# A hybrid attention layer on one core: the order of the two gated branches and the spread of the quarter sums

## The chip, the cores and the metric

The kernel runs on one core of a Trainium2 chip. The metric is the device time of one execution in microseconds, the median of the runs.

## The reference, cut to what matters

One layer of a streaming encoder for two request groups, 1024 prompt tokens and 32 sample tokens, all in fp32, with D = 1024:

```python
h = rms_norm(x, g_pre_mix)
qa, ka, va, ra, alr, qb, kb, vb, ga, gb = split_cols(h @ w_in)
oa, s_gla = gla_branch(qa, ka, va, ra, alr, ...)      # 4 heads, gated recurrence, width 1024
ob, k_rows, v_rows = attn_fn(qb, kb, vb, rel_bias)    # 8 heads, banded softmax, width 512
mix = (sigmoid(ga) * (oa @ w_br_a) + sigmoid(gb) * (ob @ w_br_b)) @ w_out
x = x + rms_norm(mix, g_post_mix)
f, conv_new = conv_ffn(rms_norm(x, g_pre_ffn), ...)
x = x + rms_norm(f, g_post_ffn)
gate = sigmoid(rms_norm(x, g_pre_ple) @ w_ple_gate)
x = x + rms_norm(gate * (pe @ w_ple), g_post_ple)
```

The change concerns the `mix` line, and a preparation for the products `h @ w_in` of the merge gates ga and gb.

## The kernel before, in words

**Products.** Everything is held with the features on the partitions, and the T = 1056 tokens along the free axis in three chunks of 352. An fp32 product is made of three TensorE passes on rounded halves: each operand is split into a high part (a copy to fp32r on ScalarE) and a low part (the difference, on VectorE or GpSimd), and `product` (L230 to L236) issues high x high (L234), low x high (L235) and high x low (L236). `split_hi_lo` (L238 to L240) splits activations: L239 on ScalarE, L240 on VectorE. `weights` (from L200) loads one weight tile of 512 KB into `raw` (L204, two buffers, issued by SP) and splits it in two halves, L213 on ScalarE and L214 on GpSimd, into four buffers each of `whi` and `wlo`, so that two weight tiles are alive.

**Order of work.** The program is written in one order, and a scheduler with a time model of its own orders the instructions of each engine, within the limits of the buffers. `tc.keep_in_program_order` pins an instruction; `low(QLOW)` gives a piece of work a low priority, `hp_if` a high one. Each engine takes its instructions strictly in order, and so does SP, which issues nearly all loads and stores: a DMA whose buffer or data is not ready holds up all that SP has behind it.

**Head pairs.** The band attention goes over four pairs of heads (loop `for hp in range(4)`, L706 on). In each, TensorE alternates between projection matmuls and the steps of the attention: scores (`two`, L550, L551), bias and the row's extreme on VectorE (L557), exponentials on ScalarE (L559), transposes (`one`, L566), their split on ScalarE (L569) and VectorE (`pt`, L570), the product with the values (`one`, L608) and its evacuation (L575). `vs` (L506) are the value rows, and `qs` (L525, L526) the split queries, whose low half GpSimd makes.

**Quarter sums.** The merge gates are computed later by a Strassen-Winograd scheme of seven products in place of eight, which needs sums of quarters of h. `quarter_sums(k)` (L681 to L704) makes them for one k of four: for each of two halves ten VectorE instructions on 128 x 264 tiles and four stores (L691, L696, L700, L704) from `tt` tiles to the DRAM tensor `d_t`. `tt` has four buffers. The table QUARTERS says after which head pair which k is made: k = 0 and 1 in the third, 2 and 3 in the fourth. They have low priority and so fill VectorE beside the attention.

**Branch stage.** It follows the merge gates, whose last matmuls end at 876.7 us of the span. `bh`, `bl` are the split halves of ob; `oa0h`, `oa0l` to `oa7h`, `oa7l` are those of oa, the low tile being loaded with the raw oa from DRAM (`d_oa`) first. Only oa0h to oa2h have room ahead of time; oa3h to oa7h lie in a pool `op` that opens when `bh` and `bl` are released. `ev` is a pool of five buffers of 128 x 1056, on which everything that comes and goes draws.

- Branch B: eight tiles n, each three chunks of four inner steps, two tiles to one weight tile. The gate d_gb[n] is loaded into an ev buffer (L1221), multiplied in on VectorE out of PSUM (L1226) and the result stored to DRAM, `d_tb` (L1227). The loads of oa (L1229) stand behind these stores by the table OA_LOADS.
- The splits of oa, chunk by chunk (L239, L240 again).
- Branch A: eight tiles n, each three chunks of eight inner steps, one weight tile each. The gate d_ga[n] (L1257) and the B result d_tb[n] (L1258) are loaded into two ev buffers; VectorE multiplies by the gate (L1269) and adds B (L1270), and the sum is split into `mh` and `ml` (L239, L240), the operand of w_out. Tile 0 is done in two parts, three inner steps for all chunks first.
- After each A tile comes `presplit(n)` (L1242 to L1249): it loads a tile of w_ple_gate (L1245), splits it on ScalarE (L1246) and VectorE (L1247), and stores both halves to the DRAM tensor `d_g` (L1248, L1249) for the end of the kernel. It takes two ev buffers.

PSUM has four buffers (`mm`) for these products, so TensorE can run up to three chunks ahead of an evacuation that is late. Then comes the stage of w_out, chunk by chunk, with mh and ml as its operands, its inner step 7 needing tile 7.

Of the kernel before, what the change touches and what calls it, by code (L numbers as in the profile page):

```python
# [11 lines left out]
F32 = mybir.dt.float32  # L12
# [5 lines left out]
P = 128  # L18
# [31 lines left out]
MS = 1  # L50
EVB = 5
QN = 2
QUARTERS = ((), (), (0, 1), (2, 3))
QLOW = 300
SLOTS = 7
LOOK = 2
PLAIN_GATES = (2, 3, 4, 5, 6, 7)
FIRST_SUMS = (2, 2, 2, 2, 4, 4, 0)
XB = 8
# [56 lines left out]
def emit(tc, a):  # L116
# [12 lines left out]
    def tl(p, shape, dt=F32, tag=None, bufs=None):  # L129
        tag = tag or nm("t")  # L130
        kw = {} if bufs is None else {"bufs": bufs}
        return p.tile(list(shape), dt, name=nm(tag), tag=tag, **kw)
# [17 lines left out]
    def ps_mm():  # L150
        return tl(psum, [P, 512], tag="mm", bufs=banks[0])
# [12 lines left out]
    def evt():  # L164
        return tl(ev, [P, T], tag="ev", bufs=EVB)
# [34 lines left out]
    def weights(src, eng=po, parts=1):  # L200
        raw = raw_weight()
        n = KT // parts
        for i in range(0, KT, n):
            dma.dma_start(raw[:, i : i + n], src[:, i : i + n])  # L204
        n = min(n, KT // 2)
        hi, lo = [], []
        with tc.high_priority():
            for i in range(0, KT, n):
                if i % (KT // 2) == 0:
                    hi.append(tl(wp, [P, KT // 2, P], F32R, tag="whi", bufs=4))  # L210
                    lo.append(tl(wp, [P, KT // 2, P], F32R, tag="wlo", bufs=4))
                b, d = slice(i, i + n), slice(i % 4, i % 4 + n)
                ac.activation(hi[-1][:, d], raw[:, b], AF.Copy)  # L213
                eng.tensor_tensor(lo[-1][:, d], raw[:, b], hi[-1][:, d], op=ALU.subtract)  # L214
        return hi, lo
# [19 lines left out]
            pe.matmul(ps, h, xl(kt), start=False, stop=False)  # L235
            pe.matmul(ps, l, xh(kt), start=False, stop=(last and i == n - 1))  # L236

    def split_hi_lo(hi, lo, src):  # L238
        ac.activation(hi, src, AF.Copy)  # L239
        ve.tensor_tensor(lo, src, hi, op=ALU.subtract)  # L240

    def log_exp():
        tc.keep_in_program_order(ac.preload_act_table_set("natural_log_exp_and_others"))
# [437 lines left out]
    def quarter_sums(k):  # L681
        a1, a2, b1, b2 = [[t[:, r].bitcast(F32) for t in (xh, xl)] for r in (k, k + HK) for _ in range(2)]
        n = HT // QN
        for j in range(QN):
            p, q = slice(j * n, (j + 1) * n), slice(HT + j * n, HT + (j + 1) * n)
            A, S = ALU.add, ALU.subtract
            t = tl(bp, [P, n], tag="tt", bufs=4)
            tc.keep_in_program_order(ve.tensor_tensor(t, a2[0][:, q], a1[0][:, p], op=S))
            ve.tensor_tensor(t, t, a2[1][:, q], op=A)
            ve.tensor_tensor(t, t, a1[1][:, p], op=S)  # L690
            dma.dma_start(d_t[0, k][:, p], t)  # L691
            t = tl(bp, [P, n], tag="tt", bufs=4)
            ve.tensor_tensor(t, b2[0][:, q], a2[0][:, q], op=S)
            ve.tensor_tensor(t, t, b2[1][:, q], op=A)
            ve.tensor_tensor(t, t, a2[1][:, q], op=S)
            dma.dma_start(d_t[2, k][:, p], t)  # L696
            u = tl(bp, [P, n], tag="tt", bufs=4)
            ve.tensor_tensor(u, t, a1[0][:, p], op=A)
            ve.tensor_tensor(u, u, a1[1][:, p], op=A)
            dma.dma_start(d_t[1, k][:, p], u)  # L700
            t = tl(bp, [P, n], tag="tt", bufs=4)
            ve.tensor_tensor(t, b1[0][:, p], u, op=S)
            ve.tensor_tensor(t, t, b1[1][:, p], op=A)
            dma.dma_start(d_t[3, k][:, p], t)  # L704
# [505 lines left out]
    banks[:] = [MODE, 8 - MODE, 0]  # L1210
    ps_one()

    OA_LOADS = ((), (0,), (1,), (2,), (3, 4), (5,), (6, 7), ())
    d_tb = tl(dram, [8, P, T], tag="d_tb")
    for n2 in range(4):
        hi, lo = weights(a["w_br_b"][n2])
        gs = {}
        for i in range(2):
            n = 2 * n2 + i
            g = evt()  # L1220
            dma.dma_start(g, d_gb[n])  # L1221
            for c in range(NC):
                s = chunk(c)
                ps = ps_mm()[:, : s.stop - s.start]
                product(ps, hi, lo, [(4 * i + k, k) for k in range(4)], lambda k: bh[:, k, s], lambda k: bl[:, k, s])
                ve.tensor_tensor(g[:, s], ps, g[:, s], op=ALU.mult)  # L1226
            dma.dma_start(d_tb[n], g)  # L1227
            for kt in OA_LOADS[n]:
                tc.keep_in_program_order(dma.dma_start(oa[kt][1].bitcast(F32), d_oa[kt]))  # L1229
    bo.release()  # L1230

    op = pool("op", side="right")
    for kt in range(3, KT):
        oa[kt][0] = tl(op, [P, T], F32R, tag=f"oa{kt}h")
    for c in range(NC):
        for kt in range(KT):
            h, l = [t[:, chunk(c)] for t in oa[kt]]
            with hp_if(c == 0):
                split_hi_lo(h, l, l.bitcast(F32))
    d_g = tl(dram, [KT, 2, P, KT, P], tag="d_g")  # L1240

    def presplit(n):  # L1242
        raw, hi = evt(), tl(ev, [P, T], F32R, tag="ev", bufs=EVB)
        raw, hi = raw[:, : KT * P], hi[:, : KT * P]
        dma.dma_start(raw.rearrange("p (k c) -> p k c", c=P), a["w_ple_gate"][n])  # L1245
        ac.activation(hi, raw, AF.Copy)  # L1246
        ve.tensor_tensor(raw.bitcast(F32R), raw, hi, op=ALU.subtract)  # L1247
        dma.dma_start(d_g[n, 0].rearrange("p k c -> p (k c)"), hi.bitcast(F32))  # L1248
        dma.dma_start(d_g[n, 1].rearrange("p k c -> p (k c)"), raw)  # L1249

    mp = pool("mp")
    mh = tl(mp, [P, KT, T], F32R, tag="mh")
    ml = tl(mp, [P, KT, T], F32R, tag="ml")
    for n in range(KT):
        hi, lo = weights(a["w_br_a"][n])
        g, t = evt(), evt()
        dma.dma_start(g, d_ga[n])  # L1257
        dma.dma_start(t, d_tb[n])  # L1258
        parts = [range(KT)] if n else [range(3), range(3, KT)]
        mms = [ps_mm()[:, : width(c)] for c in range(NC)] if n == 0 else []  # L1260
        for ks in parts[:-1]:
            for c in range(NC):
                s = chunk(c)
                product(mms[c], hi, lo, [(k, k) for k in ks], lambda k: oa[k][0][:, s], lambda k: oa[k][1][:, s], last=False)
        for c in range(NC):
            s = chunk(c)
            ps = ps_mm()[:, : s.stop - s.start] if n else mms[c]
            product(ps, hi, lo, [(k, k) for k in parts[-1]], lambda k: oa[k][0][:, s], lambda k: oa[k][1][:, s], first=n > 0)
            ve.tensor_tensor(g[:, s], ps, g[:, s], op=ALU.mult)  # L1269
            ve.tensor_tensor(g[:, s], g[:, s], t[:, s], op=ALU.add)  # L1270
            split_hi_lo(mh[:, n, s], ml[:, n, s], g[:, s])
        presplit(n)
    op.release()
    ol.release()
    ev.release()

# [1 line left out]
    d_x1 = tl(dram, [8, P, T], tag="d_x1")  # L1278
    d_hn = tl(dram, [8, P, T], tag="d_hn")

    hh, hl = mh, ml
    zp = pool("zp", side="right")
    wo = pool("wo", side="right")
# [1265 lines left out]
```

## Time and profile before

| what | value |
|---|---|
| median of 3 runs | 1911.93 us (1910.86 to 1914.52) |
| profiled execution | 1918.39 us, of which 1916.7 us span |
| mean granted TensorE clock | 0.994 |
| matmuls / weight loads on TensorE | 13484 / 13484, busy 98% of the span |
| busy share of VectorE, ScalarE, GpSimd | 70%, 47%, 23% |
| second, third, fourth head pair | 145 to 235, 235 to 325, 325 to 400 us |
| GLA branch | 400 to 760 us |
| merge gates | 760 to 876.7 us |
| branch stage | 876.7 to 1024.5 us |
| w_out, FFN, per-layer embedding | 1024.5 to 1916.7 us |

In the rows of the profile a name such as `mm<-oa3h,whi` is what an instruction writes and reads; `x24` counts the instructions of a group. PE is TensorE, PEld its weight loads, DVE VectorE, ACT ScalarE, POOL GpSimd, SP the queue that issues most DMAs. A time in brackets is how long the engine stood idle before the instruction, with what released it. A matmul of 352 columns shows some 0.33 us from start to end, but successive ones overlap, and one starts every 0.16 us at full clock; so the rate is read from counts over a stretch and not from the busy time of one.

### The profile page before, as it was taken

The numbers are of one execution on the slowest core, as the hardware profiler recorded it, in microseconds if no ns is written. First come the engines' busy times: TensorE is split into PE (matmuls) and PEld (weight loads), VectorE is DVE, ScalarE is ACT, GpSimd is POOL, SyncE is SP. The second block draws the span as 40 slices with busy tenths as digits, with TensorE's granted clock in tenths as the row PEclk, the third lists the DMA queues.
The fourth block names the chain that finished last, engine by engine and source line by source line (L and its number), as shares of the span: only waits on it lengthen the run. The fifth ranks groups of instructions, "written<-read, shape, count | busy, mean of one in ns | idle before, by whom it ended". The sixth has DMA issues, their size and how long they took to land.

```text
span 1916.7 us, 34771 instructions
## 1 busy us (share of the span) xinstructions
PE 1876.7 (98%) x13484; PEld 1843.6 (96%) x13484; DVE 1346.3 (70%) x2713; ACT 905.2 (47%) x1709; POOL 435.9 (23%) x548
## 2 busy tenths in 40 slices
PE   9999999999999999999999999999999999999997
PEld 8999989889999999999999999999999999999997
DVE  6655576668878875785554687887777766556886
ACT  7456445345454554543334554433333345444554
POOL 2313222252112221002220113332222222114312
PEclk9999999999999999999999999999999999999999
DMA  7324356452323443697785256553444348565677
GB/s 273 120 97 136 116 157 163 128 143 67 95 82 110 106 121 114 220 346 254 272 284 206 91 176 234 182 167 129 137 136 138 131 148 309 185 192 188 216 262 152
DMA packets 112419, 325.12 MB, mean 170 GB/s; under 512 B 14005, under 2 KB 35965, under 8 KB 112125
## 3 DMA queue, kind: packets, MB, share of 16 engines
q1 hardware_dynamic: 86124, 234.95, 36.7%
q0 software_dynamic: 25296, 87.04, 15.6%
q8 instruction: 106, 1.74, 0.4%
q10 hardware_dynamic: 832, 0.90, 0.1%
q14 instruction: 61, 0.49, 0.1%
HBM read 226.44 MB, written 116.25 MB: 179 GB/s over the span
## 4 chain that ended last, share of the span: by engine, by line
PE 77%; DVE 10%; DMA 4%; issue 4%; ACT 4%; POOL 1%; SPq 0%; DVEq 0%; ACTq 0%; POOLq 0%
PE c L1975 10%; PE mm L234 10%; PE mm L235 10%; PE mm L236 10%; PE two L1713 6%; PE two L1711 6%; PE two L1712 6%; PE aux L1975 2%; DMA d_tb<-ev 2%; PE mm L1082 2%; PE mm L1084 2%; PE mm L1083 2%; PE one L608 1%; PE one L566 1%; PE two L912 1%
## 5 line engine op out<-in xcount | busy, mean ns | idle before, releaser
L234 PE MATMUL mm<-xh,whi 128*128 128x352 f32 (+2 forms) x1008 | 335.0, 332 | 1.5 <-DVE q L806 0.9
L236 PE MATMUL mm<-xh,wlo 128*128 128x352 f32 (+2 forms) x1008 | 332.9, 330 | 0.0
L235 PE MATMUL mm<-xl,whi 128*128 128x352 f32 (+2 forms) x1008 | 331.0, 328 | 0.0
L214 POOL TENSOR_TENSOR wlo<-raw,whi 128x512 fp32r<-128x512 f32 x108 | 156.3, 1455 | 678.9 <-ACT whi L213 665.0
L234 PEld LDWEIGHTS mm<-xh,whi 128*128 128x128 f32 x1008 | 191.2, 190 | 4.0 <-DVE q L806 1.3
L236 PEld LDWEIGHTS mm<-xh,wlo 128*128 128x128 f32 x1008 | 190.3, 189 | 1.8 <-issue 1.0
L235 PEld LDWEIGHTS mm<-xl,whi 128*128 128x128 f32 x1008 | 190.9, 189 | 0.9
L1713 PE MATMUL two<-mh,wlo 128*128 128x264 f32 x576 | 162.8, 284 | 0.1
L1712 PE MATMUL two<-ml,whi 128*128 128x264 f32 x576 | 162.5, 283 | 0.0
L1711 PE MATMUL two<-mh,whi 128*128 128x264 f32 x576 | 161.2, 284 | 0.4 <-ACT whi L239 0.4
L1975 PE MATMUL c<-mh,whi 128*128 128x264 f32 x396 | 112.4, 284 | 0.0
L1975 PE MATMUL c<-mh,wlo 128*128 128x264 f32 x396 | 112.3, 283 | 0.0
L213 ACT ACTIVATE whi<-raw 128x512 fp32r<-128x512 f32 x116 | 71.7, 626 | 85.9 <-PE mm L235 39.8
L1975 PE MATMUL c<-ml,whi 128*128 128x264 f32 x396 | 112.2, 283 | 0.0
L1713 PEld LDWEIGHTS two<-mh,wlo 128*128 128x128 f32 x576 | 108.2, 188 | 0.3 <-DVE wlo L240 0.3
L1712 PEld LDWEIGHTS two<-ml,whi 128*128 128x128 f32 x576 | 108.3, 188 | 0.0
L1711 PEld LDWEIGHTS two<-mh,whi 128*128 128x128 f32 x576 | 107.3, 188 | 0.6 <-ACT whi L239 0.6
L1701 ACT ACTIVATE whi<-ws 128x512 fp32r<-128x512 f32 x72 | 45.3, 631 | 97.8 <-PE two L1712 64.6
L559 ACT ACTIVATE s<-s,sm 128x640 f32<-128x640 f32 (+5 forms) x72 | 50.3, 698 | 71.2 <-DVE sm L557 70.0
L234 PE MATMUL mm<-mh,ahi 128*128 128x352 f32 x240 | 77.4, 322 | 0.0
L235 PE MATMUL mm<-ml,ahi 128*128 128x352 f32 x240 | 77.4, 322 | 0.0
L236 PE MATMUL mm<-mh,alo 128*128 128x352 f32 x240 | 77.2, 322 | 0.0
(649 smaller groups left out, 5946.7 us busy)
## 6 DMA issues: line engine op xcount, KB each, us to landing
raw<-in_w_in SPq DMA_DIRECT2D x51, 512.0 KB, 3.8
uraw<-d_b POOLq DMA_DIRECT2D x33, 528.0 KB, 4.9
raw<-in_w_up SPq DMA_DIRECT2D x26, 512.0 KB, 3.6
d_b<-av POOLq DMA_DIRECT2D x44, 264.0 KB, 2.7
d_s<-in_w_down POOLq DMA_DIRECT2D x16, 704.0 KB, 7.9
draw<-d_s SPq DMA_DIRECT2D x16, 704.0 KB, 4.7
hn<-d_b POOLq DMA_DIRECT2D x40, 264.0 KB, 3.6
d_b<-hn POOLq DMA_DIRECT2D x40, 264.0 KB, 2.4
```

The lines of the kernel that those rows point to most:

```text
L213: ac.activation(hi[-1][:, d], raw[:, b], AF.Copy)
L214: eng.tensor_tensor(lo[-1][:, d], raw[:, b], hi[-1][:, d], op=ALU.subtract)
L234: pe.matmul(ps, h, xh(kt), start=(first and i == 0), stop=False)
L235: pe.matmul(ps, h, xl(kt), start=False, stop=False)
L236: pe.matmul(ps, l, xh(kt), start=False, stop=(last and i == n - 1))
L559: ac.activation(s, s, AF.Exp, scale=-1.0, bias=sm[:nq], accum_out=sums[:nq, q0 // P : q0 // P + 1])
L1082: pe.matmul(o, w[n][0][:, k], x[0][:, k, s], start=begin, stop=False, skip_group_check=True)
L1701: ac.activation(h, x, AF.Copy)
L1711: pe.matmul(ps[:, j, :HC], w[0][:, k], x[0][:, k, s], start=st, stop=False, skip_group_check=True)
L1712: pe.matmul(ps[:, j, :HC], w[0][:, k], x[1][:, k, s], start=False, stop=False, skip_group_check=True)
L1713: pe.matmul(ps[:, j, :HC], w[1][:, k], x[0][:, k, s], start=False, stop=sp_, skip_group_check=True)
L1975: pe.matmul(ps, w, x, start=st, stop=sp_, skip_group_check=True)
```

## The change

Two parts.

**Quarter sums.** QUARTERS gives k = 0 to the second head pair, 1 to the third, 2 and 3 to the fourth as before. `tt` gets twelve buffers.

**Branch stage.** The tiles of both branches come in one list ORDER: b0 to b3, a0, a1, b4, b5, a2, a3, b6, b7, a4 to a7. The B results stay in four of the five ev buffers until their A tile adds them; stores to and reloads from d_tb are gone. All A gates go through the fifth buffer, loaded by thirds (three DMAs of 176 KB a tile). All oa loads are issued at the head of the stage. mh, ml and oa3h to oa7h are allocated at once, on the other side of memory, so that they no longer wait for bh and bl to go. The splits of oa are pinned in program order: oa0 after b1, oa1 and oa2 after b2, oa3 and oa4 after b3, the rest after the first part of a0. The presplits get a pool of their own (four raw, four high buffers), which opens when bh and bl are released after b7, and come two each after a4 to a7. Line numbers of the new kernel are 6 or 7 higher up to the branch stage, and differ from there on.

```diff
@@ -50,10 +50,16 @@
 MS = 1
 EVB = 5
 QN = 2
-QUARTERS = ((), (), (0, 1), (2, 3))
+QUARTERS = ((), (0,), (1,), (2, 3))
 QLOW = 300
 SLOTS = 7
 LOOK = 2
+ORDER = ['b0', 'b1', 'b2', 'b3', 'a0', 'a1', 'b4', 'b5', 'a2', 'a3', 'b6', 'b7', 'a4', 'a5', 'a6', 'a7']
+TBN = 4
+FIRST_K = 3
+SPLITS = (0, 1, 2, 2, 0, 0, 0, 0)
+PRESPLIT = (4, 4, 5, 5, 6, 6, 7, 7)
+PREB = 4
 PLAIN_GATES = (2, 3, 4, 5, 6, 7)
 FIRST_SUMS = (2, 2, 2, 2, 4, 4, 0)
 XB = 8
@@ -235,9 +241,10 @@
             pe.matmul(ps, h, xl(kt), start=False, stop=False)
             pe.matmul(ps, l, xh(kt), start=False, stop=(last and i == n - 1))
 
-    def split_hi_lo(hi, lo, src):
-        ac.activation(hi, src, AF.Copy)
-        ve.tensor_tensor(lo, src, hi, op=ALU.subtract)
+    def split_hi_lo(hi, lo, src, pin=False):
+        ins = ac.activation(hi, src, AF.Copy), ve.tensor_tensor(lo, src, hi, op=ALU.subtract)
+        for i in ins if pin else ():
+            tc.keep_in_program_order(i)
 
     def log_exp():
         tc.keep_in_program_order(ac.preload_act_table_set("natural_log_exp_and_others"))
@@ -684,21 +691,21 @@
-            t = tl(bp, [P, n], tag="tt", bufs=4)
+            t = tl(bp, [P, n], tag="tt", bufs=12)
...
@@ -1210,67 +1217,87 @@
     banks[:] = [MODE, 8 - MODE, 0]
     ps_one()
 
-    OA_LOADS = ((), (0,), (1,), (2,), (3, 4), (5,), (6, 7), ())
-    d_tb = tl(dram, [8, P, T], tag="d_tb")
-    for n2 in range(4):
-        hi, lo = weights(a["w_br_b"][n2])
-        gs = {}
-        for i in range(2):
-            n = 2 * n2 + i
-            g = evt()
-            dma.dma_start(g, d_gb[n])
+    mp = pool("mp")
+    mh = tl(mp, [P, KT, T], F32R, tag="mh")
+    ml = tl(mp, [P, KT, T], F32R, tag="ml")
+    op = pool("op")
+    for kt in range(3, KT):
+        oa[kt][0] = tl(op, [P, T], F32R, tag=f"oa{kt}h")
+
+    def split_oa(kt):
+        for c in range(NC):
+            h, l = [t[:, chunk(c)] for t in oa[kt]]
+            split_hi_lo(h, l, l.bitcast(F32), pin=True)
+
+    kept = [evt() for _ in range(EVB)]
+    ga, tb, w_b = {}, {}, {}
+
+    def branch_b(n):
+        if n % 2 == 0:
+            w_b[n // 2] = weights(a["w_br_b"][n // 2])
+        hi, lo = w_b[n // 2]
+        g = tb[n] = kept[n % TBN]
+        dma.dma_start(g, d_gb[n])
+        for c in range(NC):
+            s = chunk(c)
+            ps = ps_mm()[:, : s.stop - s.start]
+            product(ps, hi, lo, [(4 * (n % 2) + k, k) for k in range(4)], lambda k: bh[:, k, s], lambda k: bl[:, k, s])
+            ve.tensor_tensor(g[:, s], ps, g[:, s], op=ALU.mult)
+
+    def branch_a(n):
+        hi, lo = weights(a["w_br_a"][n])
+        g = kept[TBN + n % (EVB - TBN)]
+        for c in range(NC):
+            dma.dma_start(g[:, chunk(c)], d_ga[n][:, chunk(c)])
+        parts = [range(KT)] if n else [range(FIRST_K), range(FIRST_K, KT)]
+        mms = [ps_mm()[:, : width(c)] for c in range(NC)] if n == 0 else []
+        for ks in parts[:-1]:
             for c in range(NC):
                 s = chunk(c)
-                ps = ps_mm()[:, : s.stop - s.start]
-                product(ps, hi, lo, [(4 * i + k, k) for k in range(4)], lambda k: bh[:, k, s], lambda k: bl[:, k, s])
-                ve.tensor_tensor(g[:, s], ps, g[:, s], op=ALU.mult)
-            dma.dma_start(d_tb[n], g)
-            for kt in OA_LOADS[n]:
-                tc.keep_in_program_order(dma.dma_start(oa[kt][1].bitcast(F32), d_oa[kt]))
-    bo.release()
-
-    op = pool("op", side="right")
-    for kt in range(3, KT):
-        oa[kt][0] = tl(op, [P, T], F32R, tag=f"oa{kt}h")
-    for c in range(NC):
-        for kt in range(KT):
-            h, l = [t[:, chunk(c)] for t in oa[kt]]
-            with hp_if(c == 0):
-                split_hi_lo(h, l, l.bitcast(F32))
+                product(mms[c], hi, lo, [(k, k) for k in ks], lambda k: oa[k][0][:, s], lambda k: oa[k][1][:, s], last=False)
+            late_splits()
+        for c in range(NC):
+            s = chunk(c)
+            ps = ps_mm()[:, : s.stop - s.start] if n else mms[c]
+            product(ps, hi, lo, [(k, k) for k in parts[-1]], lambda k: oa[k][0][:, s], lambda k: oa[k][1][:, s], first=n > 0)
+            ve.tensor_tensor(g[:, s], ps, g[:, s], op=ALU.mult)
+            ve.tensor_tensor(g[:, s], g[:, s], tb[n][:, s], op=ALU.add)
+            split_hi_lo(mh[:, n, s], ml[:, n, s], g[:, s])
+
     d_g = tl(dram, [KT, 2, P, KT, P], tag="d_g")
 
     def presplit(n):
-        raw, hi = evt(), tl(ev, [P, T], F32R, tag="ev", bufs=EVB)
-        raw, hi = raw[:, : KT * P], hi[:, : KT * P]
+        raw, hi = [tl(gsp, [P, KT * P], dt, tag=t, bufs=PREB) for t, dt in (("graw", F32), ("ghi", F32R))]
         dma.dma_start(raw.rearrange("p (k c) -> p k c", c=P), a["w_ple_gate"][n])
         ac.activation(hi, raw, AF.Copy)
         ve.tensor_tensor(raw.bitcast(F32R), raw, hi, op=ALU.subtract)
         dma.dma_start(d_g[n, 0].rearrange("p k c -> p (k c)"), hi.bitcast(F32))
         dma.dma_start(d_g[n, 1].rearrange("p k c -> p (k c)"), raw)
 
-    mp = pool("mp")
-    mh = tl(mp, [P, KT, T], F32R, tag="mh")
-    ml = tl(mp, [P, KT, T], F32R, tag="ml")
-    for n in range(KT):
-        hi, lo = weights(a["w_br_a"][n])
-        g, t = evt(), evt()
-        dma.dma_start(g, d_ga[n])
-        dma.dma_start(t, d_tb[n])
-        parts = [range(KT)] if n else [range(3), range(3, KT)]
-        mms = [ps_mm()[:, : width(c)] for c in range(NC)] if n == 0 else []
-        for ks in parts[:-1]:
-            for c in range(NC):
-                s = chunk(c)
-                product(mms[c], hi, lo, [(k, k) for k in ks], lambda k: oa[k][0][:, s], lambda k: oa[k][1][:, s], last=False)
-        for c in range(NC):
-            s = chunk(c)
-            ps = ps_mm()[:, : s.stop - s.start] if n else mms[c]
-            product(ps, hi, lo, [(k, k) for k in parts[-1]], lambda k: oa[k][0][:, s], lambda k: oa[k][1][:, s], first=n > 0)
-            ve.tensor_tensor(g[:, s], ps, g[:, s], op=ALU.mult)
-            ve.tensor_tensor(g[:, s], g[:, s], t[:, s], op=ALU.add)
-            split_hi_lo(mh[:, n, s], ml[:, n, s], g[:, s])
-        presplit(n)
-    op.release()
+    waiting = list(range(KT))
+
+    def late_splits():
+        while waiting:
+            split_oa(waiting.pop(0))
+
+    for kt in range(KT):
+        dma.dma_start(oa[kt][1].bitcast(F32), d_oa[kt])
+    gsp = None
+    for x in ORDER:
+        n = int(x[1])
+        if x[0] == "b":
+            branch_b(n)
+            for _ in range(SPLITS[n]):
+                split_oa(waiting.pop(0))
+            if n == KT - 1:
+                bo.release()
+                gsp = pool("gsp", side="right")
+        else:
+            branch_a(n)
+            for k in range(KT):
+                if PRESPLIT[k] == n:
+                    presplit(k)
+    gsp.release()
     ol.release()
     ev.release()
 
@@ -1278,6 +1305,7 @@
     d_x1 = tl(dram, [8, P, T], tag="d_x1")
     d_hn = tl(dram, [8, P, T], tag="d_hn")
 
+    op.release()
     hh, hl = mh, ml
     zp = pool("zp", side="right")
     wo = pool("wo", side="right")
```

ScalarE at the start of branch A, before. `oa2h<-oa2l` is a split of oa (all three chunks where it says x3), `whi<-raw` a split of weights, `ev<-ev` at L1246 a presplit.

```order
L239 ACTIVATE oa2h_10128<-oa2l_10129 128x352 x3
L213 ACTIVATE whi_10741<-raw_10739 128x512
L213 ACTIVATE whi_10745<-raw_10739 128x512
L213 ACTIVATE whi_10849<-raw_10847 128x512
L1246 ACTIVATE ev_10841<-ev_10840 128x1024
L213 ACTIVATE whi_10853<-raw_10847 128x512
L239 ACTIVATE oa3h_10680<-oa3l_10130 128x352
L239 ACTIVATE oa5h_10682<-oa5l_10132 128x352
L239 ACTIVATE oa4h_10681<-oa4l_10131 128x352
```

The same engine and place after the change, where `slot` at L1160 is a merge gate's sigmoid.

```order
L245 ACTIVATE oa2h_10128<-oa2l_10129 128x352 x3
L1160 ACTIVATE slot_9990<-slot_9990 128x1056
L1160 ACTIVATE slot_9991<-slot_9991 128x1056
L219 ACTIVATE whi_10518<-raw_10516 128x512
L219 ACTIVATE whi_10522<-raw_10516 128x512
L245 ACTIVATE oa3h_10275<-oa3l_10130 128x352 x3
L245 ACTIVATE oa4h_10276<-oa4l_10131 128x352 x3
L245 ACTIVATE oa5h_10277<-oa5l_10132 128x352 x3
L245 ACTIVATE oa6h_10278<-oa6l_10133 128x352 x3
L245 ACTIVATE oa7h_10279<-oa7l_10134 128x352 x3
```

Between the splits of oa2 and oa3 the presplit and the splits of the second weight tile are gone; all chunks of a tile are split together.

SP around a middle A tile, before: `raw` are weights, `ev<-d_ga` a gate, `ev<-d_tb` a reloaded B tile, `ev<-in_w_ple_gate` and `d_g<-ev` the presplit's load and stores.

```order
L204 DMA raw_11279<-in_w_br_a 128x1024
L1257 DMA ev_11073<-d_ga_548 128x1056
L1248 DMA d_g_10733<-ev_11057 128x1024
L1249 DMA d_g_10733<-ev_11056 128x1024
L1258 DMA ev_11074<-d_tb_10267 128x1056
L1245 DMA ev_11164<-in_w_ple_gate 128x1024
L204 DMA raw_11387<-in_w_br_a 128x1024
```

SP from a4's last gate third (L1251, first row) to a5's first (last row), after; `graw` and `ghi` are the presplit's own buffers.

```order
L1251 DMA ev_10284<-d_ga_548 128x352
L1271 DMA graw_11230<-in_w_ple_gate 128x1024
L1271 DMA graw_11237<-in_w_ple_gate 128x1024
L1271 DMA graw_11344<-in_w_ple_gate 128x1024
L1271 DMA graw_11351<-in_w_ple_gate 128x1024
L210 DMA raw_11472<-in_w_br_a 128x1024
L1274 DMA d_g_10285<-ghi_11231 128x1024
L1274 DMA d_g_10285<-ghi_11238 128x1024
L1275 DMA d_g_10285<-graw_11230 128x1024
L1274 DMA d_g_10285<-ghi_11345 128x1024
L1275 DMA d_g_10285<-graw_11237 128x1024
L1275 DMA d_g_10285<-graw_11344 128x1024
L1251 DMA ev_10284<-d_ga_548 128x352
```

Where one tile had one presplit among its loads, four presplit loads and six presplit stores now stand between two gate thirds.

More of the change, by code (lines that the diff above doesn't have):

```diff
@@ L691, in quarter_sums @@
             dma.dma_start(d_t[0, k][:, p], t)
-            t = tl(bp, [P, n], tag="tt", bufs=4)
+            t = tl(bp, [P, n], tag="tt", bufs=12)
             ve.tensor_tensor(t, b2[0][:, q], a2[0][:, q], op=S)
@@ L696, in quarter_sums @@
             dma.dma_start(d_t[2, k][:, p], t)
-            u = tl(bp, [P, n], tag="tt", bufs=4)
+            u = tl(bp, [P, n], tag="tt", bufs=12)
             ve.tensor_tensor(u, t, a1[0][:, p], op=A)
@@ L700, in quarter_sums @@
             dma.dma_start(d_t[1, k][:, p], u)
-            t = tl(bp, [P, n], tag="tt", bufs=4)
+            t = tl(bp, [P, n], tag="tt", bufs=12)
             ve.tensor_tensor(t, b1[0][:, p], u, op=S)
```

## The prediction

> **What bounds the kernel now.** I read the page first, the span and then the chain of work that ended last.
>
> ```profile
> span 1916.7 us, 34771 instructions
> ...
> PE 77%; DVE 10%; DMA 4%; issue 4%; ACT 4%; POOL 1%; SPq 0%; DVEq 0%; ACTq 0%; POOLq 0%
> ```
>
> TensorE carries three quarters of the chain. So the change can only pay where TensorE stands still or runs at half its clock, in the stretches whose order of work it alters. The next view is busy time by stretch; the columns are the stretch, its length, then busy us and instructions of PE, PEld, DVE, ACT and POOL, the granted clock, the DMA share and GB/s. The first three rows are the second, third and fourth head pair of the band attention; 876.7 to 1024.5 is the branch stage.
>
> ```profile
> 145.00:235.00 90.00, 89.75 (x613) 86.17 (x610) 52.30 (x118) 50.10 (x112) 25.17 (x22) 1.00 0.41 127
> 235.00:325.00 90.00, 85.53 (x557) 80.94 (x556) 63.14 (x151) 47.25 (x114) 24.25 (x25) 0.98 0.52 146
> 325.00:400.00 75.00, 68.63 (x447) 65.56 (x447) 50.31 (x129) 32.85 (x75) 19.53 (x27) 0.95 0.57 159
> 277.90:281.30 3.40, 3.40 (x13) 3.40 (x12) 3.17 (x12) 1.10 (x4) 0.00 (x0) 0.50 0.04 14
> 364.70:390.60 25.90, 24.45 (x173) 23.89 (x173) 12.76 (x30) 13.54 (x32) 7.89 (x12) 1.00 0.24 78
> 390.60:397.40 6.80, 5.95 (x23) 5.33 (x22) 3.34 (x10) 1.48 (x4) 4.14 (x10) 0.50 1.04 260
> 870.00:875.00 5.00, 5.00 (x44) 5.00 (x43) 5.00 (x12) 4.78 (x12) 1.17 (x2) 1.00 0.01 2
> 876.70:1024.50 147.80, 143.69 (x866) 142.54 (x866) 82.78 (x138) 44.95 (x81) 30.42 (x22) 0.98 0.80 282
> 895.00:930.00 35.00, 33.89 (x209) 33.51 (x208) 12.19 (x25) 6.65 (x14) 6.66 (x5) 1.00 0.99 349
> 933.30:940.10 6.80, 6.25 (x22) 5.79 (x21) 6.80 (x15) 4.71 (x13) 0.80 (x1) 0.50 0.99 355
> 950.00:1020.00 70.00, 70.00 (x433) 70.00 (x432) 40.28 (x62) 21.33 (x35) 14.20 (x10) 1.00 0.80 278
> ```
>
> What to see: the last row is a gapless stretch, 433 matmuls in 70.00 us, 0.1617 us each. The branch stage has 288 matmuls for branch B and 576 for A by the code (eight tiles of three chunks, 4 and 8 inner steps, three matmuls each), and 864 x 0.1617 = 139.7 us. It takes 147.8, so at most 8.1 us are to be won there without making a matmul cheaper. The second head pair loses 90.00 - 89.75 = 0.25 us to idle time, the third 4.5 and the fourth 6.4. Three stretches run at clock 0.50. The waits of TensorE name the gaps, first in 235 to 400, then in the branch stage (us in total, times, longest).
>
> ```profile
> PE two L550 <- DVE sm L557: 4.3, 4, 3.3
> PE one L608 <- DVE pt L570: 1.5, 1, 1.5
> PE one L566 <- ACT s L559: 1.5, 1, 1.5
> PE one L566 <- DVE pt L570: 1.3, 1, 1.3
> PE one L566 <- DVE vs L506: 1.1, 1, 1.1
> ```
>
> ```profile
> PE mm L234 <- ACT oa3h L239: 2.4, 1, 2.4
> PE mm L234 <- DVE ev L1226: 1.1, 1, 1.1
> PE mm L235 <- DVE oa3l L240: 0.6, 1, 0.6
> ```
>
> **Branch stage: the gaps.** The chain of waits gives the cause of the 2.4 us gap, and it is not the split itself.
>
> ```profile
> 922.53 8.00 DMA d_tb<-ev
> ...
> 930.64 1.06 ACT ev L1246
> ```
>
> The split of oa3 stood on ScalarE behind a presplit (L1246) that waited 8.00 us for a store of d_tb to free its buffer. VectorE's halves of the same splits make the 0.6. The 1.1 is VectorE standing at the split of oa0, which comes ahead of the next evacuation (L1226), until the load of oa0 lands. The change removes all three causes: no d_tb store and no reload, presplits in buffers of their own and only after a4, and all eight oa loads at the head of the stage. There they meet an empty DMA (0.01 in 870 to 875); 8 x 528 KB = 4.3 MB at the 349 GB/s of a full queue are 12.4 us, so they land by about 883, when branch B's first products run, and the splits follow from b1 on. TensorE reaches the first product with oa about 23 us into the stage, at 900. The gate loads of b1 to b3 now stand behind these 12.4 us and land at 883 to 887; b1 needs its gate at about 884.5, and four PSUM buffers let TensorE run on for three chunks (1.9 us each in branch B). So the oa loads cost nothing by this working; if that cover is gone it is rival C.
>
> Sum: 1.1 + 2.4 outside the slow stretch; inside it 22 matmuls in 6.80 us, where 3.6 would do, so 3.2 with the 0.6 gap in it. That is 6.7 of the 8.1; the other 1.4 are small steps. Of these I leave 0.8 for the end of the stage, where two splits of w_out now stand on VectorE ahead of a7's first evacuation (the nearest row is L240 below, 0.66 us each). So 8.1 - 0.8 = **7.3 us** gained.
>
> **Branch stage: what the single A gate buffer costs.** All A tiles share one buffer, reloaded by thirds. These are the steps before a third is free (mean ns last before the bar), and the DMA issues with KB each and us to landing.
>
> ```profile
> L240 DVE TENSOR_TENSOR ml<-ev,mh 128x352 fp32r<-128x352 f32 x23 | 15.1, 655 | 10.8 <-ACT mh L239 10.8
> L1270 DVE TENSOR_TENSOR ev<-ev,ev 128x352 f32<-128x352 f32 x23 | 14.8, 648 | 0.6
> L1269 DVE TENSOR_TENSOR ev<-mm,ev 128x352 f32<-128x352 f32 x23 | 11.9, 519 | 5.7 <-PE mm L236 5.7
> ```
>
> ```profile
> d_g<-ev SPq DMA_DIRECT2D x16, 512.0 KB, 2.9
> ...
> ev<-d_ga SPq DMA_DIRECT2D x8, 528.0 KB, 4.8
> ...
> raw<-in_w_br_a SPq DMA_DIRECT2D x8, 512.0 KB, 6.2
> ev<-in_w_ple_gate SPq DMA_DIRECT2D x8, 512.0 KB, 5.3
> ```
>
> Multiply 0.52, add 0.65, ScalarE's copy (about the same, estimated from these), subtract 0.66: 2.3 us, which I take as 3.0 with handovers. An A product is 72 x 0.1617 = 11.6 us, so a landing of up to 8.6 us is free, and 4.8 is the row for a whole tile. Over the three handovers from a4 to a7 the spare PSUM buffers lend another 3 x 3.9 us. Cost in the forecast: nothing.
>
> But the load on the DMA is moved. All eight presplits now fall into the last four products. Ahead of a7's first gate third SP has queued, from a4's start on, 8 loads and 16 stores of presplits, 3 weight tiles and 7 gate thirds: 27 x 512 + 7 x 176 KB = 15.4 MB. At 349 GB/s that is 44.1 us. The third's last use (w_out's first product reaching its last inner step, 3.4 us after the 46.4 us of the four products, less the 2.3 us chain) is at 47.4. It fits with 3 us to spare, but only at the full queue's rate: below 15.4 / 47.4 = 325 GB/s TensorE waits. This is rival D.
>
> **Quarter sums.** These are two of VectorE's rows in the third pair and one in the fourth, and GpSimd's row beside the second (start, length, line).
>
> ```profile
> 259.17 0.43 DVE L688 TENSOR_TENSOR tt<-xh 128x264 f32<-128x264 f32 x1 [4.43 <-DMA d_t<-tt]
> ...
> 273.59 2.55 DVE L702 TENSOR_TENSOR tt<-xh,tt 128x264 f32<-128x264 f32 x1
> ...
> 362.77 0.43 DVE L698 TENSOR_TENSOR tt<-tt,xh 128x264 f32<-128x264 f32 x1 [5.22 <-DMA d_t<-tt]
> ```
>
> ```profile
> 273.32 2.53 POOL L526 TENSOR_TENSOR qs<-ev,qs 64x1056 fp32r<-64x1056 f32 x1 [1.53 <-ACT qs L525]
> ```
>
> VectorE stood 4.43 and 5.22 us at a quarter sum because all four tt buffers were still being stored; the attention's steps queued behind it, and TensorE's gaps of 1.5 (L608) and 3.3 (L550) are these. With twelve buffers, three times as many stores must be pending before VectorE stops: both gone, 4.8 us. The 1.3 us gap follows the L702 that took 2.55 us instead of 0.43. In the third pair only one quarter k is left of two, 20 instructions of 0.43, 8.6 us less for VectorE; the second pair gets them, 52.30 + 8.6 = 61 of 90 us, as much as the third has now. I count the 1.3 as gone there and charge 0.5 to the second pair, which can meet the same collision. The stretch 277.9 to 281.3, 3.40 us at half clock right behind that gap, gives 1.7. Of what is late next the nearest row is the wait for vs (1.1): I charge 1.0. The fourth pair keeps its two quarters, and its 1.5 for ScalarE and the half clock from 390.6 stay. Sum 4.8 + 1.3 + 1.7 - 0.5 - 1.0 = **6.3 us**.
>
> The L702 row says that the two instructions overlap from start to end and both take 2.5 us. [...]
>
> Total 7.3 + 6.3 = **13.6 us**. The profiled execution took 1918.39 us, 1.7 of it outside the span and 6.5 above the median of 1911.93. Taken off it, 13.6 leaves 1904.8; since the gaps are no artefact of the profile I take the same off the median: **1898.3**.
>
> **Rivals.** A: the quarter sums give nothing. VectorE's work is the same, its gaps go elsewhere in the pairs. For it: 61 of 90 us is where the third pair stalls now. Against: the two long stalls are named as DMA waits. Gain 7.3: 1904.6.
>
> B: the half clock does not go with the gaps. For it: after the 3.3 us gap, the longest, the row 364.70 to 390.60 shows clock 1.00, while gaps of 1.3 and 2.4 were followed by 0.50; the starts 277.9, 390.6 and 933.3 lie whole multiples of about 3.41 us apart, as if windows decided. Small gaps left behind could then fall badly as well. The gain loses 3.4 + 1.7: 8.5, so 1903.4. [...]
>
> C: the oa loads at the stage's head hold up the gates of b1 to b3. b1's gate 6 us late would stop TensorE after its three chunks, and a gap there can halve the clock: 2 + 3.4, and some of the splits late too: the stage gives nothing, 1911.9 - 6.3 = 1905.6. Against: 870 to 875 is empty.
>
> D, slower: the DMA queue of a4 to a7 decides. For it: the stage ran at 282 GB/s and the last third at 278, both below 325. Against: those rows have shares of 0.80, and at 0.99 the rows show 349 and 355. At 300 GB/s 15.4 MB take 51.3 us, 3.9 late, with a half-clock window 7.3: 1905.6. At 250 they take 61.6, 14.2 late, with 3.4 of half clock 17.6: 1911.9 - 13.6 + 17.6 = 1915.9. It turns slower at 13.6 - 3.4 = 10.2 late, 57.6 us, 267 GB/s.
>
> That the change does not do what it says is excluded in the branch stage, where stores and reloads are gone from the code; for the quarters it is A.
>
> **How the numbers follow.** Forecast 0.52, A 0.13, B 0.12, C 0.07, D 0.16, half of it above the turn. About 0.2%, 3.8 us, is what a measurement of this kernel can tell from no change; faster means below 1908.1. Faster: 0.50 + 0.10 + 0.11 + 0.05 + 0.06 = 0.82; slower 0.09, nearly all D; same 0.09. Low end: all 8.1, all gaps and half clock of the third pair (6.1 + 1.7), and the fourth pair's 1.5 and 3.4 too make 20.8, 1891; I take 1892. High end: A, B, C and D at 300 GB/s lie at 1903 to 1906; 1907 takes them in and leaves out D's slow half and some tails.
>
> **What would show it.** Right: no wait for d_t or d_tb on any engine; gaps at L550 and L608 under 1 us in the second to fourth pair; the stage 140 to 141 us long at clock 1.00; a DMA share near 1 in the last 40 us of the stage and TensorE not waiting there. Wrong: a wait for a gate third or for mh and ml at the entry to w_out (D), one at b1's evacuation (C), clock 0.50 without a gap before it (B), or idle time in the three pairs still near 11 us (A).

## The result, and the profile after

The changed kernel took 1895.08 us (median of 4 runs, 1893.80 to 1897.72), the kernel before 1913.22 us (4 runs, 1910.86 to 1917.64). The ratio is 0.9904, with an interval of 0.9882 to 0.9926: 18.3 us faster, at least 14.2 and at most 22.6. The profiled execution took 1895.03 us, its span 1893.3.

The span and the chain of the changed kernel:

```profile
span 1893.3 us, 34755 instructions
...
PE 84%; DVE 7%; issue 3%; ACT 3%; DMA 1%; POOL 0%; SPq 0%; ACTq 0%; DVEq 0%; POOLq 0%
```

TensorE's share of the chain rises from 77 to 84%, that of VectorE falls from 10 to 7 and that of the DMAs from 4 to 1. Where the time came from is seen by stretches. These begin and end at the same matmuls as the rows of before: third pair, fourth pair, branch stage; the last row is a part of the last four A tiles.

```profile
234.90:317.60 82.70, 82.47 (x558) 78.99 (x558) 56.82 (x133) 46.87 (x115) 22.84 (x23) 1.00 0.51 137
317.60:385.70 68.10, 65.36 (x448) 63.08 (x447) 49.50 (x128) 33.10 (x76) 22.41 (x34) 1.00 0.63 180
862.50:1002.20 139.70, 139.70 (x868) 139.70 (x867) 80.14 (x132) 43.49 (x77) 30.69 (x22) 1.00 0.59 217
965.00:995.00 30.00, 30.00 (x189) 30.00 (x188) 21.22 (x30) 11.37 (x18) 5.68 (x4) 1.00 1.02 408
```

The two pairs together took 165 us and take 150.8; their idle time fell from 4.5 + 6.4 to 0.2 + 2.7. The branch stage has no idle time at all and takes 139.7 us, the figure worked out for a gapless stage. No stretch of the attention or the branch stage runs at half clock. What is left of TensorE's waits in 235 to 400:

```profile
PE one L573 <- ACT s L566: 1.5, 1, 1.5
PE mm L240 <- DVE q L813: 1.1, 1, 1.1
PE mm L240 <- DVE ev L856: 0.6, 1, 0.6
PE two L557 <- DVE sm L564: 0.5, 2, 0.2
```

The waits of 3.3 (scores), 1.5 (value product), 1.3 (transposes behind L570) and 1.1 (vs) are gone; the 1.5 for ScalarE is the tail of the fourth pair, at the same instruction as before.

Between the two profiled executions lie 23.4 us, between the medians 18.1. So five microseconds of this comparison belong to the one execution that was profiled, and the experiments had to say which.

### The profile page after: what moved, and what is told of

The parts are those of the page before. It is cut to its first block, busy times and chain, and to the rows that moved or that the text cites. A ratio compares the mean times of both kernels' runs of the same rounds, so it can differ in the third digit from the quotient of the medians.

```text
span 1893.3 us, 34755 instructions
## 1 busy us (share of the span) xinstructions
PE 1866.0 (99%) x13484; PEld 1836.2 (97%) x13484; DVE 1347.5 (71%) x2713; ACT 905.2 (48%) x1709; POOL 434.0 (23%) x548
## 4 chain that ended last, share of the span: by engine, by line
PE 84%; DVE 7%; issue 3%; ACT 3%; DMA 1%; POOL 0%; SPq 0%; ACTq 0%; DVEq 0%; POOLq 0%
PE mm L240 12%; PE mm L241 12%; PE mm L242 12%; PE c L2003 11%; PE two L1739 6%; PE two L1741 6%; PE two L1740 6%; PE aux L2003 2%; PE mm L1089 2%; PE mm L1091 2%; PE mm L1090 2%; PE one L615 2%; PE one L573 2%; PE two L919 1%; PE two L557 1%
```

## The experiments

### Each part alone

First the two edits to the quarter sums on the kernel before; the `tt` line stands for the four that allocate such a tile. The gains in this section follow from the ratio, which is not that of the two medians; the difference of the medians can be 1.5 us off.

```diff
-QUARTERS = ((), (), (0, 1), (2, 3))
+QUARTERS = ((), (0,), (1,), (2, 3))
-            t = tl(bp, [P, n], tag="tt", bufs=4)
+            t = tl(bp, [P, n], tag="tt", bufs=12)
```

> The kernel before with both edits to the quarter sums and nothing else. Theory 1 (the two parts are independent, and the pairs gained what the traces show): the stretch of the third and fourth pair gets 10 to 14 us shorter, the branch stage keeps its 147.8 with the gaps of 2.4 and 1.1 and its half clock; the median falls by about 10. Theory 2 (the forecast's size): 6.3. Theory 3 (the half-clock stretches fall by chance from run to run, and the profiled run of before had three): the profile gains up to 14, the median only 6 to 9.

Measured: 1901.42 against 1914.97 us, ratio 0.9937 (0.9918 to 0.9956), 12.1 us faster (8.4 to 15.7). The pairs take 154.7 us, 10.3 less than before, as Theory 1 said; the size in the forecast, 6.3, was half of what the runs gained. In the branch stage Theory 1 was wrong, and that, with the same code as before, was a surprise:

```profile
866.10:1007.20 141.10, 140.59 (x868) 140.20 (x867) 80.53 (x135) 43.89 (x79) 31.25 (x22) 1.00 0.84 295
```

It takes 141.1 us, not 147.8, at full clock. The gap before oa3 does not show; of TensorE's waits in the stage one is left, VectorE's half of that split:

```profile
PE mm L235 <- DVE oa3l L240: 0.5, 1, 0.5
```

Then the complement, the changed kernel with the quarters of before.

```diff
-QUARTERS = ((), (0,), (1,), (2, 3))
+QUARTERS = ((), (), (0, 1), (2, 3))
-            t = tl(bp, [P, n], tag="tt", bufs=12)
+            t = tl(bp, [P, n], tag="tt", bufs=4)
```

> The changed kernel with the table of quarters and the four tt buffers of before: only the branch stage is changed. Theory 1: the branch stage takes 139.7 to 140 us and the pairs are as before: 8 us faster. Rival (the half clock in the branch stage is chance): 5 us faster in the median, with the stage gapless all the same.

Measured: 1911.53 us, ratio 0.9984 (0.9974 to 0.9995), 3.1 us faster (1.0 to 5.0) and not 8. Yet the stage does what was said:

```profile
877.50:1017.40 139.90, 139.90 (x869) 139.78 (x868) 80.70 (x132) 43.37 (x76) 31.80 (x22) 1.00 0.59 216
```

So the branch change gives a gapless stage, and what it is worth depends on how long the stage usually was. The rival of this run (5 us) is nearer than Theory 1. The two parts together, 12.1 + 3.1 = 15.2, lie within the interval of the whole; the 3 us by which they fall short of its 18.3 are assigned by no run.

### The kernel before, once more

> The kernel before, profiled a second time. Theory 1 (half clock and the size of the gaps in the branch stage are chance of the run): half-clock stretches elsewhere than at 278, 391 and 933, the pairs' gaps at the same instructions with the same sizes, the branch stage 141 to 144 us as in the three runs that have it unchanged. Rival (the first profile is typical): 148 us again, with the 2.4 gap and half clock behind it.

Measured: one execution of 1913.63 us. The first row is the branch stage, the second and third the half-clock stretches of this execution.

```profile
876.30:1021.50 145.20, 142.39 (x868) 141.41 (x867) 82.00 (x137) 44.82 (x82) 30.48 (x22) 0.99 0.82 287
389.00:396.00 7.00, 6.12 (x27) 5.51 (x26) 3.60 (x12) 1.48 (x4) 4.95 (x11) 0.52 1.06 272
932.00:936.00 4.00, 3.36 (x13) 3.36 (x14) 4.00 (x10) 4.00 (x11) 0.20 (x1) 0.57 0.96 308
```

TensorE's waits in the branch stage of the same execution:

```profile
PE mm L234 <- ACT oa3h L239: 1.5, 1, 1.5
PE mm L235 <- DVE oa3l L240: 0.8, 1, 0.8
PE mm L234 <- DVE ev L1226: 0.5, 1, 0.5
```

The instructions are those of the first profile, the sizes are not: 1.5 for 2.4, 0.8 for 0.6, 0.5 for 1.1, and the half clock behind them lasts about half as long (3.42 us for 6.82). The 2.4 us gap had followed a d_tb store of 8.00 us; here the chain has, in the same place,

```profile
923.00 5.64 DMA d_tb<-ev
```

In one point Theory 1 was wrong: half clock does not stand elsewhere, but behind the same two gaps as at 391 and 933; only the stretch at 278 is missing. The theory's 141 to 144 was missed by 1.2 us, the rival's 148 by 2.8. With the two quarter experiments below the same code of the branch stage was seen in five executions:

```profile
869.20:1011.80 142.60, 141.16 (x868) 140.18 (x867) 80.43 (x134) 43.93 (x79) 31.63 (x22) 1.00 0.83 291
```

```profile
872.70:1016.20 143.50, 141.11 (x869) 140.24 (x868) 80.55 (x135) 43.82 (x79) 31.25 (x22) 1.00 0.83 289
```

141.1, 142.6, 143.5, 145.2 and 147.8, on average 144.0. The first profile is the slowest of the five. Against 139.8 the branch change is worth 4.2 us by this average, and 1.3 to 8.0 by single executions.

### Buffers or spread

Twelve buffers alone, then the spread alone, on the kernel before.

```diff
-            t = tl(bp, [P, n], tag="tt", bufs=4)
+            t = tl(bp, [P, n], tag="tt", bufs=12)
```

> The kernel before with twelve tt buffers, the sums still two and two in the third and fourth pair. Theory 1 (the stores of d_t hold up VectorE): no wait for d_t, the gaps of 1.5 (value product) and 3.3 (scores) are gone, 5 us faster; the 1.3 behind a quarter sum beside GpSimd stays. Rival (too much VectorE work in the third pair, buffers do not matter): under 2 us, the gaps move.

Measured: 1907.12 us, ratio 0.9954 (0.9941 to 0.9967), 8.8 us faster. No instruction waits for a store of d_t any more. TensorE's waits in 235 to 400:

```profile
PE one L566 <- ACT s L559: 1.5, 1, 1.5
PE one L566 <- DVE vs L506: 1.1, 1, 1.1
PE one L629 <- DVE pt L570: 1.1, 1, 1.1
PE two L550 <- DVE sm L557: 0.9, 2, 0.6
...
```

The 3.3 and the 1.5 at the value product are gone, as Theory 1 said; of the 1.3 a 1.1 is left at another product, again behind a quarter sum of 2.50 us (L703). The gain is larger than the 5 expected.

```diff
-QUARTERS = ((), (), (0, 1), (2, 3))
+QUARTERS = ((), (0,), (1,), (2, 3))
```

> The kernel before with the sums over three pairs and four tt buffers as before. Theory 1: the fourth pair is as before, its 5.2 us wait for d_t and the 3.3 gap stay; the third pair loses its 1.3 gap and perhaps the 1.5: 2 to 4.5 us faster. Rival (the crowding decides): 8 to 12 us faster, all that the two quarter edits give together.

Measured: 1910.47 us, ratio 0.9977 (0.9964 to 0.9989), 4.4 us faster. First TensorE's waits in 235 to 400, then VectorE's waits for the stores:

```profile
PE two L550 <- DVE sm L557: 3.4, 3, 3.0
PE one L608 <- DVE pt L570: 3.1, 2, 1.6
...
```

```profile
DVE tt L688 <- DMA d_t<-tt: 9.0, 2, 4.5
...
DVE tt L698 <- DMA d_t<-tt: 5.0, 1, 5.0
```

The stall of 5.0 in the fourth pair and its gap of 3.0 stay, and the stall of 4.5 comes twice: spreading the sums does not remove the stalls while a second set of stores must wait for four buffers. What it removes are the 1.3 behind a quarter sum and the 1.1 for vs. Buffers give two thirds, the spread one third (8.8 + 4.4 against 12.1); the rival, that crowding decides, falls.

### What stood ahead of the oa3 split

The kernel before, each presplit three A tiles later; stores and reloads of d_tb stay.

```diff
-        presplit(n)
+        if n >= 3:
+            presplit(n - 3)
+    for n in range(KT - 3, KT):
+        presplit(n)
```

> The kernel before with each presplit made three A tiles later, so that none stands on ScalarE ahead of the splits of oa; d_tb is still stored and reloaded. Theory 1 (the gap before oa3 is a presplit that waits for a store's buffer): no wait for oa3 on TensorE, the branch stage 140 to 141 us, 2 to 4 us faster, as much as the whole branch change. Rival (the full DMA delays the loads of oa, whatever stands on ScalarE): gaps of 0.5 to 2.4 stay, now released by the load of oa3 to oa7, stage 141 to 144 us.

Measured: 1915.53 us, ratio 1.0008 (0.9998 to 1.0018): no faster. TensorE's waits from the branch stage into w_out, and the chain ahead of the longer one:

```profile
PE mm L234 <- ACT ahi L1295: 5.3, 1, 5.3
PE mm L234 <- DVE ev L1226: 0.9, 1, 0.9
```

```profile
1030.51 6.63 DMA d_g<-ev
...
1037.16 0.38 SPq L1362
...
1039.13 6.73 DMA raw<-in_w_out
```

The wait for oa3 is gone and the stage takes 141.6 us. The queue is as full as before in the stretch that shows 349 GB/s there:

```profile
895.00:930.00 35.00, 34.10 (x211) 33.81 (x210) 16.42 (x33) 10.82 (x25) 7.96 (x6) 1.00 0.98 352
```

So the presplit on ScalarE was the cause, and the theory of a full DMA delaying oa's loads falls. But the three presplits now at the end hold up SP: it waits 6.63 us for one of their stores before it can issue the loads of L1362, w_out's weights stand behind these, and TensorE waits 5.3 us for the weights, with a stretch of half clock (0.51 over 1044 to 1051). The gain is given back 23 to 28 us after the stage. What the changed kernel adds to this edit is room: the presplits' own buffers, so that they fit ahead of the stage's end.

### The DMA load of a4 to a7

The changed kernel with every half of a presplit stored twice.

```diff
+    d_g2 = tl(dram, [KT, 2, P, KT, P], tag="d_g2")
...
         dma.dma_start(d_g[n, 1].rearrange("p k c -> p (k c)"), raw)
+        dma.dma_start(d_g2[n, 0].rearrange("p k c -> p (k c)"), hi.bitcast(F32))
+        dma.dma_start(d_g2[n, 1].rearrange("p k c -> p (k c)"), raw)
```

> The changed kernel with every presplit half stored twice, the second time to another DRAM tensor: 8.4 MB more between a4 and a7. Forecast's working of rival D with the rate that the changed kernel showed there (15.4 + 8.4 = 23.8 MB at 410 GB/s are 58 us against 47.4): TensorE waits about 11 us for a7's gate or for the operand of w_out, 11 to 14 us slower than the changed kernel. Rival (the stores do not hold up the gate thirds): under 3 us slower.

Measured: 1907.37 us, 12.3 above the changed kernel, in the range of the working. TensorE's wait, VectorE's row that ends it (in brackets what VectorE waited for), and two stretches, the queue and the half clock:

```profile
PE mm L240 <- ACT mh L245: 8.3, 1, 8.3
```

```profile
1012.22 0.53 DVE L1263 TENSOR_TENSOR ev<-mm,ev 128x352 f32<-128x352 f32 x1 [8.72 <-DMA ev<-d_ga]
```

```profile
965.00:1012.00 47.00, 40.31 (x249) 39.72 (x247) 22.18 (x32) 12.18 (x20) 6.13 (x4) 0.97 1.03 412
1009.00:1020.00 11.00, 6.12 (x22) 5.85 (x23) 2.64 (x6) 2.00 (x4) 0.00 (x0) 0.54 0.92 367
```

a4 starts 93.1 us into the stage (576 matmuls of b0 to b7 and a0 to a3 at 0.1617), here at 955.1, and the evacuation waits for a7's first gate third until 1012.2: 57 us, where 23.8 MB at 410 GB/s are 58. That the two are so close is in part luck. By the trace 27 of the 32 stores stood ahead of that third and not all, and over these 57.1 us the queue moved 22.6 MB, 395 GB/s. The rival, that the stores do not hold up the gate, falls.

### One quarter sum in each pair

The changed kernel with all four pairs used.

```diff
-QUARTERS = ((), (0,), (1,), (2, 3))
+QUARTERS = ((0,), (1,), (2,), (3,))
```

> The changed kernel with one quarter sum in each of the four head pairs. Theory 1 (after the change the pairs' gaps come from the tail of the fourth pair, not from VectorE's sums): within 2 us of the changed kernel, the gaps of 1.5 and 1.1 at the end of the fourth pair stay. Rival (VectorE's load still makes them): they shrink, 2 to 5 us faster, since half clock goes with them.

Measured: 1897.10 us, 2.0 above the changed kernel's 1895.08; against before 0.9913 (0.9897 to 0.9928). TensorE's two waits of the tail stay:

```profile
PE one L573 <- ACT s L566: 1.2, 1, 1.2
PE mm L240 <- DVE q L813: 0.9, 1, 0.9
```

Less work on VectorE there shortens the first by 0.25 us. The second was 1.1 in the first profile of the changed kernel and is 0.9 in its second one too, so its 0.2 is no effect of this edit. Half clock followed here as well, for 6.8 us from 380.1. No version better than the changed kernel follows from the runs.

### The changed kernel, once more

> The changed kernel, profiled a second time. Theory 1 (half clock is chance of the run, and only gaps can start it): the same three gaps in the fourth pair and behind it (1.5, 1.1 and 0.6), the branch stage 139.7 to 140 us again; half clock either nowhere or behind one of these gaps, the time then 3 us longer, as in the one of four runs with clock 0.995 (1897.72 against 1893.8 to 1895.1). Rival (the changed order is safe from half clock): none, clock 0.998.

Measured: one execution of 1897.83 us. The same stretch, behind the same gap of 1.45 us, first in this execution and then in the first profile of the same kernel:

```profile
380.00:387.00 7.00, 6.10 (x23) 5.48 (x23) 3.53 (x11) 1.48 (x4) 5.39 (x16) 0.52 1.02 260
```

```profile
380.00:387.00 7.00, 6.10 (x37) 6.10 (x38) 3.91 (x13) 0.77 (x2) 5.45 (x19) 1.00 1.04 272
```

The program, the gap and the busy time are the same, the clock is 0.52 in one and 1.00 in the other, and 23 matmuls are begun where 37 were. The two executions differ by 2.8 us, and so does the fourth pair with its tail (70.9 us for 68.1). The rival falls: the changed order is not safe from half clock. What decides between the two, no run shows.

## Why the prediction was right, and where it was not

The time lay in the range and the sign was right; the gain was 18.3 us where 13.6 were forecast. But the two terms were wrong in opposite directions: 7.3 for the branch stage measured 3.1, and 6.3 for the quarter sums measured 12.1. That the sum came as near as it did is in part luck.

**Branch stage: the step that failed is the one from the profiled execution to the median.** The forecast said that "since the gaps are no artefact of the profile I take the same off the median". The mechanism was right: presplit, late oa and the splits made the gaps (the presplit by experiment, the other two by their rows alone), and the stage became gapless at 139.7. But the size of the oa3 gap hangs on when a store of d_tb lands (8.00 us for the 2.4, 5.64 for the 1.5), and how long half clock lasts behind it, if it comes at all, differs from run to run. The same code took 141.1 to 147.8 us; the profiled execution was the slowest of five, and stood 6.5 us above the median in the forecast's own figures (3.4 above the 1914.97 of 29 later runs, so that the median of three was itself low). That surplus was noted and then not used.

**Quarter sums: two charges that were not due, and half clock.** The forecast counted 6.1 us of gaps and took 1.5 off for a collision in the second pair and for what is late next. Nothing was late next: idle time in 235 to 400 fell from 10.8 to 3.0 us, 7.8 for 4.6. The wait for vs went too, with the spread and not with the buffers: twelve buffers alone left it at 1.1, and with the spread alone it was gone. The second pair showed no loss in any run. The collision did move there, as the forecast allowed, and cost TensorE nothing. These are VectorE's and GpSimd's rows in the second pair of the changed kernel, where TensorE's idle time is 0.25 us as before:

```profile
178.09 1.97 DVE L709 TENSOR_TENSOR tt<-xh,tt 128x264 f32<-128x264 f32 x1
177.22 2.54 POOL L683 TENSOR_TENSOR ev<-ev,ev 128x1056 f32<-128x1056 f32 x1 [8.28 <-PE one L615]
```

L709's median in this kernel is 0.43 us. That GpSimd's instruction makes this one longer is read from the overlap; no run here isolates it. Much of the rest of the 12.1 is half clock, which was put at 1.7. In the kernels with the sums as before, half clock stood in the third and fourth pair in each of four profiles, about 7 to 14 us of it; with both edits it was absent in two profiles (the changed kernel and the twice-stored one) and there in two others (both edits alone, the changed kernel again) for 7 to 10 us. On average over these four and four profiles, the two pairs took 165.2 and 152.7 us, idle time 11.2 and 3.0, half clock 10.2 and 4.3. So 8.2 of the 12.5 us are idle time; 6.0 us less at half clock are worth 3.0, by an estimate from the granted 0.50, and the last 1.3 stay open. This size is argued from a handful of profiles, not shown by an experiment that sets the clock.

**The oa loads at the head of the stage** cost nothing, as worked out: SP issued them at 854.1 to 857.3, ahead of the stage's first matmul at 862.5, and TensorE waited for no gate. Rival C is out.

**The single A gate and the load of a4 to a7.** The row 965 to 995 shows the queue full at 408 GB/s, more than the 349 taken, and TensorE had no wait. The 16 stores and 8 loads did stand ahead of a7's first third, as counted (the working's 47.4 should read 47.5, which changes nothing). Doubling the stores put the cost where the working had it, so rival D was a real limit that this kernel stays inside of. The end of the stage, charged at 0.8, cost about 0.1. Here are VectorE's rows there in the changed kernel:

```profile
1002.84 0.69 DVE L220 TENSOR_TENSOR wlo<-raw,whi 128x512 fp32r<-128x512 f32 x1 [1.24 <-ACT whi L219]
1003.45 0.52 DVE L1263 TENSOR_TENSOR ev<-mm,ev 128x352 f32<-128x352 f32 x1
```

a7's first evacuation does stand behind a split of w_out's weights, as the order said; its last step (L245, at 1005.10, 0.53 long) ends at 1005.6, when TensorE asks for it. There is no room left at this place: any more work there would show.

**Rival A** is out: the idle time did not move, it went. **Rival B** was half right. A gap does not always bring half clock: the 1.45 us gap at the fourth pair's tail was followed by it in seven of ten profiles and not in three, the 3.3 to 3.7 us gap at L550 in neither profile of the kernel before, but in two other runs that have the same quarter sums. But its sign, clock 0.50 without a gap before it, did not appear: from the second pair to the end of the branch stage every stretch of half clock in the eleven profiles began within 4.4 us of the start of a gap of 1.1 us or more. And it was wrong that the loss would stay: where there are fewer gaps there is less of it (4.3 us of half clock for 10.2, as above). That windows decide, which it took from three starts, no run shows.

## What to carry to other kernels

A profiled execution is one draw. Before its gaps are priced, compare its time with the median, and where it stands well above, profile the kernel again: a wait that ended with a DMA (2.4 and 1.5 us ahead of the oa3 split) and the half clock behind it (6.82 and 3.42 us) varied here from run to run, while a stall of an engine behind its own buffers came back at the same place (5.22, 5.3 and 5.0 us in the fourth pair of three kernels with four tt buffers). A buffer count that lets stores finish behind the engine was worth more here, 8.8 us, than the spread (4.4) or the branch order (3.1). And work put off from a crowded place was paid where it landed, with 5.3 us in the run of late presplits: add up the bytes that the queue must carry ahead of the next load that someone waits for, at the rate that a full queue shows in the trace (408 to 412 GB/s here).

## What the runs showed of the hardware that was not expected

- The clock fell to 0.50 behind gaps of TensorE of 1.1 to 1.5 us in some executions, and stayed at 1.00 behind the same gap in others; a gap of 3.7 us in the second profile of the kernel before passed without it. From the second pair up to the last 10 us of the kernel the stretches lasted 3.41, 6.83 or 10.24 us. Within one profile their starts lie whole multiples of 3.413 us apart: in the first profile of the kernel before they are 277.92, 390.56 and 933.28, which is 33 and 159 times that, in its second one 389.34 and 932.06, again 159 times, and so in every other profile that has more than one.
- At the fourth pair's tail the clock fell in eight profiles (one of them the kernel with one sum in each pair, whose gap is 1.2 us), 2.4 to 4.0 us after the gap had begun: in the two profiles of the kernel before 3.18 and 2.77 us after it, in the second one of the changed kernel 3.68 us. In three it did not fall. So the same program can have either. The length of the gap alone does not explain it: it was 1.45 us in both profiles of the changed kernel, and the clock fell in one of them. What decides was not shown, nor whether the light work behind the gap counts as well.
- 16 DMA engines carried 408 to 412 GB/s over 30 to 47 us where most of the traffic was presplit stores and weight tiles, against 349 over 35 us of the branch stage of the kernel before, and at most 379 over any 30 us (3 to 33) and 359 over any 47 us (818 to 865) of that kernel.
